# Attention stage of a hybrid encoder block: output-projection weights asked for two jobs ahead, residual rows one per unit, the first position table in its own pool

## The chip, the cores and the metric

The kernel runs on one core of one Trainium2 chip. The metric is the device time of one execution in microseconds (us), the median of three runs. Engines are named as in the profile: PE (TensorE matmul), DVE (VectorE), ACT (ScalarE), POOL (GpSimd) and SP (SyncE, which here only issues DMAs). Line numbers (L1020) are those of the kernel before.

## The reference, cut to what matters

One encoder layer over 1024 tokens of width 1024. One input projection feeds two groups of heads. The mLSTM group (4 heads of 128) gives `y_a`, the neighbourhood attention (8 heads of 64 on a grid of 16 rows by 64 columns, window 8 by 16) gives `y_b`; then come the output projection with the residual, an MLP and a gated embedding.

```python
s = jnp.einsum('bhcd,bhrcwd->bhcrw', q_row, k_win).astype(jnp.float32)
s = s + bias.transpose(0, 2, 1, 3)[None]          # rpb: learned position bias
prob = jax.nn.softmax(...)                        # over the 8 x 16 window
y_b = jnp.einsum('bhcrw,bhrcwd->bhcd', prob, v_win)
...
h = h + jnp.einsum('bse,ed->bsd', jnp.concatenate([y_a, y_b], axis=-1), w_out[i])
z = jnp.einsum('bsd,df->bsf', rms_norm(h, norm2_g[i]), w_ff1[i])
```

All products are made from fp32 values split into a high and a low part, with three matmuls for each product (`passes`).

## The kernel before, in words

The stages follow one another: input projections, mLSTM (pool `m1`), attention (pool `m2`), MLP, gate. The change lies in the attention stage, and in two lines at the end of the mLSTM stage.

The attention is cut into 32 units: `n = 8 pr + 4 rb + cb`, with four pairs of heads (`pr`), two row blocks and four column blocks. The order of the stage is written out by hand (`tc.manual_schedule()`, from L1102) and is pipelined by one unit. Unit n of the loop issues, in this order: `scores(n+1)` (six matmuls, L936), `values(n-1)` (twelve matmuls, L986), `prep_tiles(n)` (loads of the next pair's raw k and q rows, L836, and of its value tile `vw`, L894), `exps(n+1)` (DVE adds the position table to the scores and takes the extreme, L944; ACT the exponential, L945), `tab_load(n+5)` (the table five units ahead), `prep(n)` (in units 3, 4, 5, 9, 11 and so on: the next pair's k and q rows are normed on DVE, L817, with a small product `nb` on PE), a first portion of fill matmuls, `transposes(n)` (L966), the copies of the transposed probabilities (L973, L975) and the normalisation of unit n+1 (L950, L955, L957), and a second portion of fill matmuls.

A position table is a tile of 12 x 2 x 32 floats on 128 partitions. It comes in two DMAs (L923): half of the partitions from `tabI`, issued on SP, the other half from `tabU`, issued on POOL, and a memset on POOL (L924). In DRAM both are read as 4 x 16 pieces. Five tables are held (`TABS`), so table n+5 waits until `exps(n)` has read its buffer. The first table is loaded when the pool `m2` opens, in memory that the mLSTM stage has just left.

The fill matmuls are the output projection of the features that are ready (`out_part`, L1014), taken one at a time from the generator `fill_jobs`. There are six jobs: jobs 0 to 2 multiply the four mLSTM features (48 matmuls each), jobs 3 to 5 the first three attention features (36 each, possible from unit 24 on). FILLA and FILLB say how many are taken per portion, by pair of heads; the fill starts in unit 4. A job's weights `wo_...` are loaded by `w_raw` (L1020, on SP, three buffers) when the job before it starts, and split into high and low part by `w_split` (ACT L137, DVE L140) after that job's twelfth matmul. Both engines work in order, so a split that waits for its load holds up all that is behind it.

Beside that the first units hold: the last five row blocks of a v projection (`run(nv1, ...)`, 24 matmuls each, L309, and a store L342), the high/low split of the four mLSTM features (`y_split`, L1039 and L1040, units 2 and 3), and the loads of the residual rows (`out_res`, L1029, two at a time in units 2, 3 and 9).

SP issues its DMAs in program order, and each waits until the DMA issued eight before it on SP has landed (the eight completion counters go round), besides waiting for the buffer that it writes.

Of the kernel before, what the change touches and what calls it, by code (L numbers as in the profile page):

```python
# [18 lines left out]
P = 128  # L19
# [15 lines left out]
NV1 = 3  # L35
TABS = 5
PCS = 5
FILLA = (4, 4, 3, 7)
FILLB = (4, 4, 3, 7)
PREP0 = (0, 1, 2)  # L40
TBC = (1, 2, 3, 4)
ORD = ('n0', 'm1', 'n1', 'm2', 'n2', 'm3', 'n3', 'm0')
# [16 lines left out]
def tile_block(ctx, tc, xT, pT, w_in, w_out, w_ff1, w_ff2, w_gate, w_up, vecs, gate_b, rpbp, con,  # L59
# [391 lines left out]
    def run(it, n=None):  # L451
        for i, _ in enumerate(it):
            if n is not None and i == n - 1:
                return
# [222 lines left out]

    y_m = []
    aa, MP, wpv, wj, enm = (gk[n] for n in ("aa", "MP", "wpv", "wj", "enm"))
    m1p_ctx = tc.tile_pool(name="m1p", bufs=1, space=PSUM)  # L680
    m1p = m1p_ctx.__enter__()
    with tc.tile_pool(name="m1", bufs=2) as m1:

        heads = {}
# [183 lines left out]
        for h in range(4):  # L868
            mlstm_sweeps(h)
            if h == 0:  # L870
                na_ssq(7)
            if h < 3:
                mlstm_front2(h + 1)
                run(o0) if h == 0 else run(o1, 5) if h == 1 else run(o1)
            if h < 2:
                mlstm_front(h + 2)
            if h == 2:
                nv1 = proj_nv(1)
        run(nv1, NV1)
        with after("tk"):  # L880
            mlstm_finish(3)
# [7 lines left out]
    with tc.tile_pool(name="m2", bufs=2) as m2, tc.tile_pool(name="m2p", bufs=2, space=PSUM) as m2p:  # L889
# [7 lines left out]
        hres = {}  # L897


        NU = 32  # L900
        g3 = lambda t_: t_.rearrange("p (r c) -> p r c", c=64)
        heads2 = (slice(0, 64), slice(64, 128))
        tabs, scs, sms, pts, pvs, vws, ys = {}, {}, {}, {}, {}, {}, {}

        def geom(n):
            pr, u = divmod(n, 8)
            rb, cb = divmod(u, 4)
            return pr, rb, cb, KW[cb], 12 * KW[cb]

        def tab_load(n):  # L910
            if n >= NU:
                return
            pr, rb, cb, kw, w_ = geom(n)
            tab = m2.tile([P, 12, 2, 32], F32, tag="tab", name=f"tab{n}", bufs=TABS)
            tab = tab.rearrange("p a s b -> p (a s b)")[:, : 2 * w_]
            io, bo = (0, 64) if rb == 0 else (64, 0)
            r_0, a0, dead = (4, 0, 8) if rb == 0 else (0, 4, 0)
            k0 = (64 if cb > 1 else 0) + 16 * pr
            for q_, tb, p0, r0, c0, nr in ((nc.sync, tabI, io, 0, 0, 12), (nc.gpsimd, tabU, bo, r_0, a0, 8)):
                tb = tb[min(cb, 3 - cb)]  # L920
                src = bass.AP(tb.tensor, tb.offset + k0 * 30 * kw + r0 * 2 * kw,
                              [[2 * kw, 4], [30 * kw, 16], [1, nr * 2 * kw]])
                q_.dma_start(tab[p0 : p0 + 64, c0 * 2 * kw : (c0 + nr) * 2 * kw], src)  # L923
            G.memset(tab[bo : bo + 64, dead * 2 * kw : (dead + 4) * 2 * kw], NEG)  # L924
            tabs[n] = tab.rearrange("p (a s b) -> p s a b", s=2, b=kw)

        def scores(n):

# [94 lines left out]
        def w_split(raw, es, ks):  # L1023
            h_, l_ = split(wp, raw, raw.shape[1], "w", f"wo{ks[0]}_{es[0]}")
            return [t_.rearrange("p (k n) -> p k n", k=len(ks)) for t_ in (h_, l_)]
# [16 lines left out]
            ylo.append(b)  # L1042

        JOBS = [((e, e + 1), ks) for ks in (range(0, 4), range(4, 7)) for e in (0, 2, 4)]
        raws, ws_ = {}, {}

        def fill_jobs():
            for i, (es, ks) in enumerate(JOBS):
                if i + 1 < len(JOBS):
                    raws[i + 1] = w_raw(*JOBS[i + 1])  # L1050
                n = 0
                while len(yhi) <= ks[-1]:
                    yield
                for _ in out_proj(es, ks, mmps, ws_.pop(i)):
                    n += 1
                    if n == 12 and i + 1 < len(JOBS):
                        ws_[i + 1] = w_split(raws.pop(i + 1), *JOBS[i + 1])
                    yield

        fills = fill_jobs()  # L1060

# [38 lines left out]
                nat[pr + 1][2] = m2q(pr + 1, 0)  # L1100

        with tc.manual_schedule():  # L1102
            for n in range(TABS):
                tab_load(n)
                if n == 1:
                    vws[0] = load_vw(0)
            raws[0] = w_raw(*JOBS[0])
            scores(0)
            exps(0)
            for s in range(2):  # L1110
                recip(0, s)
                norm(0, s)
            for n in range(NU):
                if n + 1 < NU:
                    scores(n + 1)
                if n:
                    values(n - 1)
                prep_tiles(n)
                if n + 1 < NU:
                    exps(n + 1)  # L1120
                tab_load(n + TABS)
                begun = late[:]
                late.clear()
                for it in begun:
                    next(it, None)
                prep(n)
                for it in late:
                    next(it)
                if n:
                    values_out(n - 1, False)  # L1130
                if n < 4:
                    run(nv1, 1 if n < 2 else None)
                    if n > 1:
                        y_split(2 * n - 4)
                else:
                    fill(FILLA[n // 8])
                transposes(n)
                pt_copy(n, 1)
                if n + 1 < NU:
                    recip(n + 1, 0)  # L1140
                    norm(n + 1, 0)
                pt_copy(n, 0)
                if n + 1 < NU:
                    recip(n + 1, 1)
                    norm(n + 1, 1)
                if n:
                    values_out(n - 1, True)
                if n < 4:
                    run(nv1, 1) if n < 2 else None
                    if n > 1:  # L1150
                        y_split(2 * n - 3)
                    if n == 2:
                        ws_[0] = w_split(raws.pop(0), *JOBS[0])
                else:
                    fill(FILLB[n // 8])
                if n in (2, 3, 9):
                    e0 = {2: 0, 3: 2, 9: 4}[n]
                    out_res(e0)
                    out_res(e0 + 1)
            values(NU - 1)  # L1160
            values_out(NU - 1, False)
            values_out(NU - 1, True)
            run(fills)
    pj_ctx.__exit__(None, None, None)


# [497 lines left out]
```

## Time and profile before

| | us |
|---|---|
| median of 3 runs | 1435.9 (1429.86 to 1440.37) |
| the profiled execution | 1438.19 |
| its span, first to last instruction | 1436.4 |
| PE busy in the span | 1315.8 (92%) |
| attention stage, first scores to the start of unit 24 | 425.85 to 585.25 |

Times in the trace are us from the span's start. A "unit start" is the first `sc` matmul on L936 that the unit issues: unit 0 at 432.37 (its scores are those of unit 1), unit 7 at 494.53, unit 24 at 585.25. [...]

### The profile page before, as it was taken

Reading aid. Unit: us, or ns where it says so; the run is one execution under the profiler, and the core shown is the slowest. Engines: PE = TensorE matmul, PEld = TensorE weight load, DVE = VectorE, ACT = ScalarE, POOL = GpSimd, SP = SyncE. Lnnn points to the kernel's source line nnn. Section 1 sums busy time; section 2 is a strip of 40 time slices with the busy share of each in tenths; the row PEclk is TensorE's granted clock in tenths of the full one; section 3 lists DMA queues with packets and bytes.
Section 4 is the critical chain, followed back from the end, with each engine's and each line's share of the span. In section 5 each row is a group of like instructions: output and inputs, shape, how many; then the busy total and the mean of one; then the engine's idle time right before and its main releaser. Section 6 shows DMA issues by size and latency. Waiting matters only on the chain.

```text
span 1436.4 us, 19458 instructions
## 1 busy us (share of the span) xinstructions
PE 1315.8 (92%) x7055; PEld 1096.4 (76%) x7055; DVE 974.9 (68%) x1491; ACT 615.3 (43%) x1019; POOL 607.9 (42%) x481
## 2 busy tenths in 40 slices
PE   7999999999988669996999999999998899996887
PEld 6988777899877547774778888887886678885765
DVE  4487786665663436679756666666559987677788
ACT  7353443455554435545432333334333335445432
POOL 2215675553431213217266656653214640056654
PEclk9999999999998879998999999999999999998998
DMA  8543333565225544311244555446966754530152
GB/s 280 194 147 94 106 116 106 173 213 159 96 79 153 146 123 112 111 45 44 69 139 145 161 162 161 153 147 219 325 195 219 222 176 134 173 90 29 59 174 89
DMA packets 155344, 206.06 MB, mean 143 GB/s; under 512 B 20848, under 2 KB 104880, under 8 KB 155248
## 3 DMA queue, kind: packets, MB, share of 16 engines
q1 hardware_dynamic: 142480, 182.10, 40.4%
q10 hardware_dynamic: 7200, 13.11, 2.7%
q0 software_dynamic: 5568, 9.61, 2.3%
q8 instruction: 55, 0.90, 0.3%
q14 instruction: 41, 0.34, 0.1%
HBM read 151.60 MB, written 53.17 MB: 143 GB/s over the span
## 4 chain that ended last, share of the span: by engine, by line
PE 53%; DVE 11%; DMA 7%; issue 5%; POOL 4%; ACT 2%; SPq 0%; DVEq 0%; POOLq 0%; ACTq 0%
PE f_P L1364 14%; PE p_s_t L255 9%; PE p L255 5%; PE op L1014 4%; PE p_s L255 3%; PE p_t L255 3%; PE o0p L309 2%; PE pv L986 2%; PE o1p L309 1%; DMA wo_4r<-w_out 1%; PE pt L966 1%; PE num L754 1%; PE g_s L1489 1%; DMA tab<-tabI 1%; PE sc L936 1%
## 5 line engine op out<-in xcount | busy, mean ns | idle before, releaser
L1253 DVE TENSOR_TENSOR zl<-zr,zh 128x1024 fp32r<-128x1024 f32 x56 | 84.7, 1519 | 6.2 <-ACT zh L1252 6.2
L255 PE MATMUL p<-b,w_ah 128*128 128x512 f32 x256 | 80.4, 396 | 3.5 <-DVE b L192 3.5
L955 POOL TENSOR_SCALAR pc<-pc,st 128x288 f32<-128x288 f32 (+1 forms) x32 | 17.4, 542 | 150.6 <-DVE st L950 91.7
L1234 POOL TENSOR_TENSOR w2re<-sk,w2re 128x512 f32<-128x512 f32 x16 | 27.0, 1687 | 100.2 <-issue 69.1
L259 DVE TENSOR_TENSOR z<-z,p_s_t 128x512 f32<-128x512 f32 x64 | 42.5, 685 | 32.4 <-PE p_s_t L255 31.1
L1252 ACT ACTIVATE zh<-zr 128x1024 fp32r<-128x1024 f32 x56 | 58.2, 1047 | 11.7 <-DMA zr<-zd 10.8
L255 PEld LDWEIGHTS p<-b,w_ah 128*128 128x128 f32 x256 | 49.0, 192 | 14.1 <-DVE b L192 3.9
L1364 PE MATMUL f_P<-zl,w2h 128*128 128x512 f32 x128 | 51.8, 405 | 8.4 <-DVE zl L1253 8.4
L255 PE MATMUL p<-b,w_al 128*128 128x512 f32 x128 | 50.9, 399 | 7.6 <-DVE w_al L140 7.6
L986 PE MATMUL pv<-pT,vw 128*64 128x128 f32 (+1 forms) x384 | 30.1, 295 | 29.1 <-DVE pT L975 29.1
L945 ACT ACTIVATE pc<-pc,st 128x288 f32<-128x288 f32 (+1 forms) x64 | 36.3, 569 | 46.9 <-DVE st L944 46.9
L944 DVE CUSTOM_DVE_ANT_1 pc<-sc,tab 128x288 f32<-128x288 f32 (+1 forms) x64 | 29.9, 504 | 38.8 <-POOL pc L955 14.8
L1387 POOL TENSOR_TENSOR h<-h,evP 128x512 f32<-128x512 f32 x8 | 14.3, 1822 | 98.4 <-ACT evP L1378 98.4
L1277 POOL TENSOR_TENSOR tz<-z,z 128x512 f32<-128x512 f32 x16 | 20.7, 1296 | 82.4 <-ACT z L1266 82.4
L758 POOL TENSOR_SCALAR wv<-vh,wj 128x129 f32<-128x129 f32 x56 | 30.5, 549 | 56.1 <-PE num L759 50.8
L1364 PE MATMUL f_P<-zh,w2h 128*128 128x512 f32 x128 | 50.5, 394 | 1.1 <-ACT zh L1252 1.1
L1364 PE MATMUL f_P<-zh,w2l 128*128 128x512 f32 x128 | 50.4, 394 | 0.0
L1265 DVE SCALAR_TENSOR_TENSOR z<-z,Rb 128x1024 f32<-128x1024 f32 x32 | 49.3, 1547 | 0.9 <-ACT Rb L179 0.9
L986 PEld LDWEIGHTS pv<-pT,vw 128*64 128x64 f32 (+1 forms) x384 | 21.8, 144 | 36.6 <-DVE pT L975 30.6
L137 ACT ACTIVATE w_bh<-w_0r 128x1024 fp32r<-128x1024 f32 x16 | 17.0, 1062 | 74.4 <-POOL w_0r L233 54.7
L137 ACT ACTIVATE w_ah<-w_0r 128x1024 fp32r<-128x1024 f32 x16 | 17.0, 1062 | 68.4 <-PE p_t L255 68.4
L255 PE MATMUL p_s_t<-bt,w_bh 128*128 128x512 f32 x128 | 41.9, 410 | 3.4 <-ACT w_bh L137 3.4
(874 smaller groups left out, 4787.0 us busy)
## 6 DMA issues: line engine op xcount, KB each, us to landing
zr<-zd SPq DMA_DIRECT2D x56, 512.0 KB
zd<-z ACTq DMA_DIRECT2D x48, 256.0 KB
w2r<-w_ff SPq DMA_DIRECT2D x48, 256.0 KB
w_0r<-w_ff SPq DMA_DIRECT2D x16, 512.0 KB
w_1r<-w_ff SPq DMA_DIRECT2D x16, 512.0 KB
zd<-tz SPq DMA_DIRECT2D x32, 256.0 KB
zd<-z SPq DMA_DIRECT2D x32, 256.0 KB
w2re<-w_ff SPq DMA_DIRECT2D x16, 512.0 KB
```

Of the source, the lines that this page charges most:

```text
L137: mark["hi"] = S.activation(hi, raw, AF.Copy).ins
L255: TE.matmul(ps, x_, y_, start=j == 0 and i == 0, stop=j == 3 and i == 2)
L259: mark["add"] = V.tensor_tensor(o, a, b, op=ALU.add).ins
L309: mm = TE.matmul(ps[:, :256], a, b, start=k == 0 and i == 0, stop=k == KT - 1 and i == 2)
L758: G.tensor_scalar(wv, vh[:, c, 0:129], wj[:, col], 1.0, op0=ALU.mult, op1=ALU.mult)
L945: S.activation(pb, pb, AF.Exp, scale=-1.0, bias=st[:, 0:1], accum_out=st[:, 1:2])
L986: TE.matmul(pv[e0 : e0 + 64, cb], vws[pr][: 4 * kw, cb, rb + j, e0 : e0 + 64], pT[s][: 4 * kw, j], start=j == 0, stop=j == 2)
L1014: TE.matmul(ps, a, b, start=n == 0 and i == 0, stop=n == len(ks) - 1 and i == 2)
L1252: S.activation(hi, raw, AF.Copy)
L1253: dv.append(V.tensor_tensor(lo, raw, hi.bitcast(F32), op=ALU.subtract).ins)
L1265: V.scalar_tensor_tensor(z_, z_, 0.0, Rb, op0=ALU.max, op1=ALU.mult)
L1364: pe_last = TE.matmul(ps[n, e], a, b, start=st and k == 0, stop=sp and k == 2)
```

## The change

Job weights are loaded two jobs ahead: job 0's in unit 1, job 1's in unit 4, job 2's in unit 6, and each later one when the weights of the job two before it are split. A new function `job_weights`, called once per unit after the fill, makes the split when the running job has given at least twelve matmuls. The fill starts in unit 7 (NJ) with ten matmuls per unit, then ten in units 8 to 15, eight in units 16 to 23. The v projection's last five blocks are spread over units 0 to 3 (two, one, one, one), the four feature splits over units 3 to 6, and the residual rows are loaded one at a time in units 4, 5, 6, 7, 9 and 10. The first table has a pool of its own, opened before the mLSTM stage, and is loaded there; tables 5, 10, 15 ... use the same buffer, the others the remaining four. The `tabU` half of every table is issued on SP instead of POOL.

```diff
-FILLA = (4, 4, 3, 7)
-FILLB = (4, 4, 3, 7)
+FILLA = (5, 5, 4, 7)
+FILLB = (5, 5, 4, 7)
+NJ = 7
...
+    tb0_ctx = tc.tile_pool(name="tb0", bufs=1)
...
     def tab_load(n):
-            tab = m2.tile([P, 12, 2, 32], F32, tag="tab", name=f"tab{n}", bufs=TABS)
+        pool, tag, bufs = tabp[0] if n % TABS else (tb0, "tab0", 1)
+        tab = pool.tile([P, 12, 2, 32], F32, tag=tag, name=f"tab{n}", bufs=bufs)
...
-            for q_, tb, p0, r0, c0, nr in ((nc.sync, tabI, io, 0, 0, 12), (nc.gpsimd, tabU, bo, r_0, a0, 8)):
+        for q_, tb_, p0, r0, c0, nr in ((nc.sync, tabI, io, 0, 0, 12), (nc.sync, tabU, bo, r_0, a0, 8)):
...
             if h == 2:
                 nv1 = proj_nv(1)
+                tab_load(0)
...
         def fill_jobs():
             for i, (es, ks) in enumerate(JOBS):
-                if i + 1 < len(JOBS):
-                    raws[i + 1] = w_raw(*JOBS[i + 1])
-                n = 0
                 while len(yhi) <= ks[-1]:
                     yield
+                done[0] = 0
                 for _ in out_proj(es, ks, mmps, ws_.pop(i)):
-                    n += 1
-                    if n == 12 and i + 1 < len(JOBS):
-                        ws_[i + 1] = w_split(raws.pop(i + 1), *JOBS[i + 1])
+                    done[0] += 1
                     yield
+                cur[0] += 1
+
+        def job_weights():
+
+            i = cur[0] + 1
+            if done[0] >= 12 and i in raws and i not in ws_:
+                ws_[i] = w_split(raws.pop(i), *JOBS[i])
+                if i + 2 < len(JOBS):
+                    raws[i + 2] = w_raw(*JOBS[i + 2])
...
-            for n in range(TABS):
+            for n in range(1, TABS):
+                if n == 2:
+                    vws[0] = load_vw(0)
                 tab_load(n)
-                if n == 1:
-                    vws[0] = load_vw(0)
-            raws[0] = w_raw(*JOBS[0])
...
                 if n < 4:
-                    run(nv1, 1 if n < 2 else None)
-                    if n > 1:
-                        y_split(2 * n - 4)
-                else:
+                    run(nv1, 1 if n < 3 else None)
+                if n >= NJ:
                     fill(FILLA[n // 8])
...
-                if n < 4:
-                    run(nv1, 1) if n < 2 else None
-                    if n > 1:
-                        y_split(2 * n - 3)
-                    if n == 2:
-                        ws_[0] = w_split(raws.pop(0), *JOBS[0])
-                else:
+                if n < 1:
+                    run(nv1, 1)
+                if n >= NJ:
                     fill(FILLB[n // 8])
-                if n in (2, 3, 9):
-                    e0 = {2: 0, 3: 2, 9: 4}[n]
-                    out_res(e0)
-                    out_res(e0 + 1)
+                if 3 <= n < 7:
+                    y_split(n - 3)
+                if n == 6:
+                    ws_[0] = w_split(raws.pop(0), *JOBS[0])
+                job_weights()
+                if n in (1, 4, 6):
+                    j = {1: 0, 4: 1, 6: 2}[n]
+                    raws[j] = w_raw(*JOBS[j])
+                if n in (4, 5, 6, 7, 9, 10):
+                    out_res({4: 0, 5: 1, 6: 2, 7: 3, 9: 4, 10: 5}[n])
```

SP's queue before, from the second pair of residual rows on (`tab_4804` is table 9, `wo_2r` the weights of job 1, `h` residual rows, `nvd` the last v store):

```order
L342 DMA nvd<-nv1t_4680 128x2x128
L1029 DMA h_4711<-xT 128x1024
L1029 DMA h_4713<-xT 128x1024
L923 DMA tab_4739<-tabI_111 64x1x576
L1029 DMA h_4778<-xT 128x1024
L1029 DMA h_4780<-xT 128x1024
L923 DMA tab_4804<-tabI_112 64x1x768
L1020 DMA wo_2r<-w_out 128x4x256
L923 DMA tab_4876<-tabI_112 64x1x768
```

The same place of SP's queue in the changed kernel (`tab_4783` is table 9):

```order
L343 DMA nvd<-nv1t_4738 128x2x128
L708 DMA tab_4783<-tabI_112 64x1x768
L708 DMA tab_4783<-tabU_114 64x1x512
L1029 DMA wo_2r<-w_out 128x4x256
L1038 DMA h_4825<-xT 128x1024
L708 DMA tab_4852<-tabI_112 64x1x768
L708 DMA tab_4852<-tabU_114 64x1x512
L1038 DMA h_4888<-xT 128x1024
L708 DMA tab_4912<-tabI_111 64x1x576
L708 DMA tab_4912<-tabU_113 64x1x384
```

The load of job 1's weights still stands right behind table 9. The four residual loads that stood ahead of it now stand behind it, and every table has a second DMA on this queue.

ACT before, unit 5 (`pc_0_4868` holds the scores of unit 6, `pT_1_4908` the transposed probabilities of unit 5):

```order
L945 ACTIVATE pc_0_4868,st_0_4869<-pc_0_4868,st_0_4869 128x384
L945 ACTIVATE pc_1_4872,st_1_4873<-pc_1_4872,st_1_4873 128x384
L830 ACTIVATE qh_0_4866<-nr_4641 128x512
L137 ACTIVATE wo_2h<-wo_2r 128x1024
L973 ACTIVATE pT_1_4908<-pt_1_4904 128x384
L957 ACTIVATE pc_0_4868<-pc_0_4868,st_0_4869 128x384
```

ACT in the changed kernel, unit 8 (`pc_0_5014` holds the scores of unit 9):

```order
L954 ACTIVATE pc_0_5014,st_0_5015<-pc_0_5014,st_0_5015 128x384
L954 ACTIVATE pc_1_5018,st_1_5019<-pc_1_5018,st_1_5019 128x384
L1007 ACTIVATE yh_4799<-pv_1_4835 128x4x8x16
L982 ACTIVATE pT_1_5042<-pt_1_5038 96x384
L966 ACTIVATE pc_0_5014<-pc_0_5014,st_0_5015 128x384
L138 ACTIVATE wo_2h<-wo_2r 128x1024
```

The split of job 1's weights moved from the middle of unit 5 to the end of unit 8, behind the copies and the normalisation of its unit.

## Rows read from the trace of the kernel before

**Rows 1.** Chain that ended last, 395 to 540: start us, us, what.

```profile
425.64 5.79 DMA tab<-tabU
...
444.05 10.68 DMA nvd<-nv1t
...
460.95 14.51 DMA tab<-tabI
...
475.47 11.23 DMA wo_2r<-w_out
...
511.30 16.80 DMA wo_4r<-w_out
```

**Rows 2.** Waits, 414 to 540: who waited for whom, total us, times, longest.

```profile
ACT wo_4h L137 <- DMA wo_4r<-w_out: 12.2, 1, 12.2
...
ACT wo_2h L137 <- DMA wo_2r<-w_out: 9.1, 1, 9.1
```

**Rows 3.** PE's timeline: start us, us, engine, line, operation [idle before <- releaser].

```profile
432.37 1.06 PE L936 MATMUL sc<-kh,q 64*128 64x384 f32 x2 [5.86 <-DVE st L944]
...
489.62 1.55 PE L986 MATMUL pv<-pT,vw 128*64 128x128 f32 x12 [10.11 <-DVE pT L975]
...
494.53 0.40 PE L936 MATMUL sc<-kh,qh 64*128 64x288 f32 x2
...
498.65 0.45 PE L936 MATMUL sc<-kh,qh 64*128 64x384 f32 x2
...
531.01 1.55 PE L986 MATMUL pv<-pT,vw 96*64 96x128 f32 x12 [13.09 <-DVE pT L975]
...
581.61 0.40 PE L936 MATMUL sc<-kh,qh 64*128 64x288 f32 x2
...
585.25 0.45 PE L936 MATMUL sc<-kh,qh 64*128 64x384 f32 x2
```

**Rows 4.** Windows of 3 us: PE, PEld, DVE, ACT, POOL busy (x), PEclk, DMA share, GB/s.

```profile
429.00:432.00 3.00, 0.00 (x0) 0.00 (x0) 0.15 (x1) 0.00 (x0) 1.01 (x3) 0.50 0.78 185
432.00:435.00 3.00, 2.63 (x10) 2.11 (x11) 1.69 (x9) 1.65 (x6) 1.13 (x3) 0.50 0.28 84
480.00:483.00 3.00, 0.00 (x0) 0.00 (x0) 0.00 (x0) 0.00 (x0) 0.00 (x0) 0.91 0.26 94
483.00:486.00 3.00, 0.00 (x0) 0.00 (x0) 0.00 (x0) 0.00 (x0) 0.00 (x0) 0.50 0.27 89
507.00:510.00 3.00, 3.00 (x27) 2.12 (x26) 1.69 (x7) 1.69 (x5) 1.47 (x3) 1.00 0.96 243
519.00:522.00 3.00, 0.00 (x0) 0.00 (x0) 0.00 (x0) 0.00 (x0) 0.00 (x0) 0.66 0.26 101
540.00:543.00 3.00, 3.00 (x27) 2.50 (x24) 2.80 (x8) 2.17 (x7) 0.00 (x0) 1.00 0.27 66
```

**Rows 5.** DMA issues, 380 to 660: what, queue, count, KB each, median us to landing (POOL's).

```profile
tab<-tabI SPq DMA_DIRECT2D x16, 192.0 KB
tab<-tabI SPq DMA_DIRECT2D x16, 144.0 KB
tab<-tabU POOLq DMA_DIRECT2D x16, 128.0 KB, 6.5
vw<-nvd SPq DMA_DIRECT2D x8, 256.0 KB
tab<-tabU POOLq DMA_DIRECT2D x16, 96.0 KB, 5.7
vw<-nvd SPq DMA_DIRECT2D x8, 192.0 KB
```

**Rows 6.** SP's queue, 404 to 540: start us, us, line, what, count.

```profile
500.29 2.43 SPq L894 DMA_DIRECT2D vw<-nvd  x4
```

**Rows 7.** DVE's timeline, first reduction of scores in units 1 and 23, as rows 3.

```profile
447.49 0.56 DVE L944 CUSTOM_DVE_ANT_1 pc<-sc,tab 128x384 f32<-128x384 f32 x1 [7.59 <-PE pt L966]
...
582.40 0.46 DVE L944 CUSTOM_DVE_ANT_1 pc<-sc,tab 128x288 f32<-128x288 f32 x1 [0.99 <-POOL pc L955]
```

More of the change, by code (lines that the diff above doesn't have):

```diff
@@ L679, in tile_block, with geom, tab_load @@
     aa, MP, wpv, wj, enm = (gk[n] for n in ("aa", "MP", "wpv", "wj", "enm"))
+    tb0_ctx = tc.tile_pool(name="tb0", bufs=1)
+    tb0 = tb0_ctx.__enter__()
     m1p_ctx = tc.tile_pool(name="m1p", bufs=1, space=PSUM)
     m1p = m1p_ctx.__enter__()
+    NU = 32
+    tabs, tabp = {}, []
+    def geom(n):
+        pr, u = divmod(n, 8)
+        rb, cb = divmod(u, 4)
+        return pr, rb, cb, KW[cb], 12 * KW[cb]
+    def tab_load(n):
+        if n >= NU:
+            return
+        pr, rb, cb, kw, w_ = geom(n)
+        pool, tag, bufs = tabp[0] if n % TABS else (tb0, "tab0", 1)
+        tab = pool.tile([P, 12, 2, 32], F32, tag=tag, name=f"tab{n}", bufs=bufs)
+        tab = tab.rearrange("p a s b -> p (a s b)")[:, : 2 * w_]
+        io, bo = (0, 64) if rb == 0 else (64, 0)
+        r_0, a0, dead = (4, 0, 8) if rb == 0 else (0, 4, 0)
+        k0 = (64 if cb > 1 else 0) + 16 * pr
+        for q_, tb_, p0, r0, c0, nr in ((nc.sync, tabI, io, 0, 0, 12), (nc.sync, tabU, bo, r_0, a0, 8)):
+            tb_ = tb_[min(cb, 3 - cb)]
+            src = bass.AP(tb_.tensor, tb_.offset + k0 * 30 * kw + r0 * 2 * kw,
+                          [[2 * kw, 4], [30 * kw, 16], [1, nr * 2 * kw]])
+            q_.dma_start(tab[p0 : p0 + 64, c0 * 2 * kw : (c0 + nr) * 2 * kw], src)
+        G.memset(tab[bo : bo + 64, dead * 2 * kw : (dead + 4) * 2 * kw], NEG)
+        tabs[n] = tab.rearrange("p (a s b) -> p s a b", s=2, b=kw)
     with tc.tile_pool(name="m1", bufs=2) as m1:
@@ L897, in tile_block @@
         hres = {}
-        NU = 32
         g3 = lambda t_: t_.rearrange("p (r c) -> p r c", c=64)
         heads2 = (slice(0, 64), slice(64, 128))
[L903 to L913, printed above, removed]
-            tab = m2.tile([P, 12, 2, 32], F32, tag="tab", name=f"tab{n}", bufs=TABS)
[L915 to L918, printed above, removed]
-            for q_, tb, p0, r0, c0, nr in ((nc.sync, tabI, io, 0, 0, 12), (nc.gpsimd, tabU, bo, r_0, a0, 8)):
[L920 to L925, printed above, removed]
+        tabp.append((m2, "tab", TABS - 1))
+        scs, sms, pts, pvs, vws, ys = {}, {}, {}, {}, {}, {}
         def scores(n):
@@ L1044, in tile_block @@
         JOBS = [((e, e + 1), ks) for ks in (range(0, 4), range(4, 7)) for e in (0, 2, 4)]
-        raws, ws_ = {}, {}
+        raws, ws_, done, cur = {}, {}, [0], [0]
         def fill_jobs():
             for i, (es, ks) in enumerate(JOBS):
-                if i + 1 < len(JOBS):
-                    raws[i + 1] = w_raw(*JOBS[i + 1])
-                n = 0
                 while len(yhi) <= ks[-1]:
                     yield
+                done[0] = 0
                 for _ in out_proj(es, ks, mmps, ws_.pop(i)):
-                    n += 1
-                    if n == 12 and i + 1 < len(JOBS):
-                        ws_[i + 1] = w_split(raws.pop(i + 1), *JOBS[i + 1])
+                    done[0] += 1
                     yield
+                cur[0] += 1
[5 more added lines that the diff above has]
+                    raws[i + 2] = w_raw(*JOBS[i + 2])
         fills = fill_jobs()
@@ L1162, in tile_block @@
             values_out(NU - 1, True)
-            run(fills)
+            for _ in fills:
+                job_weights()
+    tb0_ctx.__exit__(None, None, None)
     pj_ctx.__exit__(None, None, None)
```

## The prediction, made before the run

> **What bounds the stage now.** I read the chain of waits first. In the attention stage it is not made of PE work alone: five DMA pieces stand in it [rows 1]. The list of waits names the two that the change speaks of, ACT's splits of the weights `wo_2` and `wo_4`, 9.1 and 12.2 us [rows 2]. PE's timeline gives what they cost there: 10.11 and 13.09 us of idle PE, and 5.86 us more in front of unit 0, where DVE waits for the first table (its POOL half landed 5.79 us after its issue) [rows 1, 3]. Between the stalls PE sets the pace: unit 7 takes 4.12 us with eight fill matmuls, unit 23 3.64 us with six, so a fill costs 0.24 us; units 7 to 23 took 4.57 us each in the mean, the second stall left out [rows 3].
>
> Then I asked why those loads take 11.23 and 16.80 us to land [rows 1], and read the windows. While PE stood idle for `wo_2`, the DMA engines were busy at a share of 0.26 and 0.27 and moved 94 and 89 GB/s; for `wo_4` it was 0.26 and 101 GB/s. With residual rows and weights in flight the share was 0.96 at 243 GB/s [rows 4]. A share that stays near 0.25 is four of the 16 engines at work. With only tables asked for on SP (540 to 543) it is 0.27 as well [rows 4]. So the tables and, by the same share in 432 to 435, the value tiles run on four engines, and the weights' last pieces wait there behind them. While the POOL halves of the first five tables landed (429 to 432) the share was 0.78 [rows 4]: those were spread wider.
>
> I take from this a sum for the four engines. What runs on them alone moves at 96 GB/s (the windows at 94, 89 and 101). A DMA of 512 KB over all 16 engines costs them between 1.33 us (a quarter of its bytes at 96) and 2.9 us. The upper end is from `wo_4`: from the issue of the value tile at 500.29 [rows 6] to 528.10 are 27.8 us; less 1.7 us of start and end, 12.8 us for 1232 KB of tile and tables, and 1.8 us for POOL's table halves, 11.5 us are left for four such DMAs. I take 2.0, near the 2.1 us that 512 KB take at the 243 GB/s of the busy window.
>
> The sum tried on the kernel before: up to `wo_2` the queue holds tables 0 to 9 (1680 KB of `tabI`), two value tiles (each 2 x 192 and 2 x 256 KB [rows 5], 1792 KB together) and 9.5 DMAs' worth of 512 KB: 427 + 3472/96 + 19 + 1 = 483.2, where 427 is the first data, 1.4 us after the first table issue, and 1 us is the completion. It landed at 486.70. The 3.5 us missing are the ten POOL halves, which use these engines too.
>
> **The change part by part.**
>
> *Weights and splits.* The two waits of rows 2 go if the loads land before their new place. The load of `wo_2` keeps its place in the queue (behind table 9), but is needed at the end of unit 8. By the sum it lands at 427 + (2560 + 1792)/96 + 5.25 x 2.0 + 1 = 483.8 (tables 1 to 9, two value tiles). Unit 5 goes on at 472.5 (below), and three and a half units at 4.57 us later unit 8 ends at about 488. `wo_4` lands at 427 + (3120 + 1792)/96 + 8.25 x 2.0 + 1 = 495.7 and is needed at the end of unit 12, four units later, about 507. So these waits cost nothing more: at most 23.2 us are free.
>
> *Fill moved.* 24 fill matmuls leave units 4 to 6 and come back in units 7 to 22: 5.8 us of PE that move. Without them units 3 to 6 are paced by DVE and by loads. The feature splits (1.2 us of DVE each) are spread over them, no work is added.
>
> *The first table early.* It is loaded in the mLSTM stage, beside PE work; I cost it at nothing there. Bounds: nothing, and 2.5 us if a load of that stage waits behind its 240 KB. Unit 0 then starts near 427.5 instead of 432.37. What is late next is table 2: in the kernel before DVE takes up the scores of unit 2 at 447.49, 4 us after PE has made them. The row puts that to PE, but no work of that unit needs the transposes; table 2 is what is left. Changed, it lands at 427 + 1536/96 + 1 = 444. So of the 4.9 us won in unit 0, 3.5 are still there in unit 1.
>
> *The second half of the tables on SP.* This is the part that speaks against the change. It takes 32 issues off POOL, which is not on the path, and puts 96 or 128 KB per table [rows 5] on the queue whose four engines are the slow ones. The trace has no `tabU` on SP; the nearest row is `tabI`, read in the same 4 x 16 pieces. At `tabI`'s rate a table costs 2.5 or 3.3 us of the four engines instead of 1.5 or 2.0 and POOL's 0.35. If SP spread it like POOL does, it would cost 1.9 or 2.4. I take the first, since it is the same shape on the same queue.
>
> [...]
>
> *SP as a queue.* Each SP DMA waits for the one eight before. With 32 more this means about 11 us from issue to landing at the rate above; tables are issued five units (over 20 us) ahead, so it holds nothing back as long as the four engines keep up.
>
> *The sum.* Needed until unit 23 can reduce its scores is table 24. In the queue up to it: tables 1 to 24, 12 x 320 + 12 x 240 = 6720 KB; four value tiles, 3584 KB; and 9472 KB over all engines (six loads of k and q rows, six of residual rows, three weights of 512 KB, three of 384, five stores of 128), 18.5 x 512 KB. 10304/96 = 107.3 and 18.5 x 2.0 = 37.0: it lands at 427 + 107.3 + 37.0 + 1 = 572.3. Two reductions follow and unit 24 starts at 573.6, against 585.25 [rows 3]; in the kernel before DVE began these reductions at 582.40 [rows 7]. On the way the waits fall after each value tile: q rows in unit 5 at 472.5, in unit 13 at 525.7, in unit 21 at 565.8. From 525.7 PE alone, ten units at 4.57 us, would reach unit 24 at 571.4: both paces end together. From unit 24 on both kernels do the same, at 14 fills per unit, paced by PE.
>
> So 11.7 us are won: 1438.2 - 11.7 = 1426.5 for an execution like the profiled one, which lies 2.3 us above the median; against the median 1435.9 - 11.7 = 1424.
>
> **The rivals.**
>
> *The queue does not pace the stage.* If SP spreads the second halves, or the four engines are faster than the windows say, nothing takes the place of the three waits: 5.86 + 10.11 + 13.09 = 29 us less, 1407. For it: after unit 13 the kernel before shows no long wait for a DMA. Against it: 0.26 at 94 and 89 GB/s with all compute engines idle, so the queue alone was late there.
>
> *The queue becomes the bound and is slower than summed.* With both halves on one queue the four engines have work from 427 to 572 without a gap. If they run at the 84 GB/s of 432 to 435 [rows 4], and a DMA over all engines costs them 2.9 us, the sum grows by 122.7 - 107.3 + 18.5 x 0.9 = 32 us, and the time is 1456: the wait has moved from the weights to the tables and the k and q rows. It turns slower than before where the 144.3 us of service grow by more than 11.7, that is by 8%. For it: `wo_4`'s 2.9 us, and that busy engines are slow (243/16 = 15 GB/s each, against 24 when four work). Against it: the engines also lose POOL's packets, and the check on `wo_2` came out within 3.5 us.
>
> *The waits on weights stay in part*, because `wo_2` lands after unit 8: its margin is only 4 us. This is within the forecast, since tables 9 and 10 are as late then.
>
> **How the numbers follow.** The forecast has 0.58, the first rival 0.27, the slower one 0.15. The forecast's own range: at 1.33 us per DMA the sum is 12 us shorter, but PE's pace holds the gain at some 23 us (1413); at 2.9 us it is 17 us longer (1441). The range reaches from 1404, a little past the first rival, to 1441; the end of the slower rival is left out. A measurement of this kernel tells about 1% from no change, that is 14.4 us. Faster by more has the first rival nearly whole and some 0.2 of the forecast where the four engines do better than 2.0: 0.46. Slower by more is the far third of the slower rival: 0.06. Within 1%: 0.48.
>
> **What would show it.** Right: no ACT wait of several us for `wo_2` or `wo_4`, no 5.86 us ahead of unit 0; long DMA pieces in the chain that end in tables or k and q rows, in units 1, 5, 13 and 21; a DMA share seldom under 0.25 between 427 and 570; unit 24 near 574. The first rival shows as units 7 to 22 at PE's pace throughout, and unit 24 before 560. The slower one shows as DVE waiting for a table in nearly every unit. I would be wrong in the mechanism if unit 1 took up its scores before 440, or if two halves of a table on SP showed a share of 0.5.

## Result: 1421.9 us, 14 us less, and the profile after

| | before | after |
|---|---|---|
| median of 5 runs, us | 1435.9 (1429.9 to 1440.4) | 1421.9 (1420.7 to 1424.5) |
| the profiled execution, its span | 1438.2, 1436.4 | 1421.5, 1419.7 |
| PE busy between 427 and 570 | 108.5 | 126.5 |
| scores of unit 24, of unit 31 after the first scores | 155.8, 192.1 | 143.6, 179.9 |

The ratio is 0.9906, 95% interval 0.9878 to 0.9935, which is 9 to 18 us less; forecast were 1424 and 11.7 us. Since the stage starts at different times in different executions (last section), I count inside it from the middle pass of the first scores (`sc<-kl`, 426.08 before, 425.98 after) and call this stage time. "Scores of unit n" is the stage time of the same pass in unit n. At the scores of unit 31 the changed kernel is 12.3 us ahead (192.13 - 179.87). The two spans differ by 16.7; the other 4.3 us come after these scores, in code that the change hardly touches, and are of the size by which executions differ there (last section).

The chain of the changed kernel, 395 to 600 us (start, us, what), which answers to [rows 1]:

```profile
430.04 13.53 DMA tab<-tabU
...
458.99 12.32 DMA nr<-qnd
...
509.71 13.98 DMA nr<-qnd
...
550.10 12.59 DMA tab<-tabU
```

The weights are gone from the chain. In their place stand two tables and two loads of q rows (`nr`), all four asked for on SP behind a value tile: a late transfer again, but another one. The list of waits (414 to 540, total us, times, longest) has no wait for a weight's load any more [rows 2]; what comes first among the DMAs is

```profile
DVE pc L953 <- DMA tab<-tabU: 18.0, 4, 10.0
...
POOL pc L964 <- DMA nr<-qnd: 7.1, 1, 7.1
...
DVE nr L847 <- DMA nr<-qnd: 5.4, 3, 3.7
```

PE's timeline, with the idle time before a row in brackets, answers to [rows 3]:

```profile
425.98 0.29 PE L945 MATMUL sc<-kl,q 64*128 64x288 f32 x2
...
427.06 0.82 PE L945 MATMUL sc<-kh,q 64*128 64x384 f32 x2 [0.66 <-DVE st L953]
...
444.35 1.08 PE L945 MATMUL sc<-kh,q 64*128 64x288 f32 x2 [2.79 <-DVE st L953]
...
521.94 0.88 PE L945 MATMUL sc<-kh,qh 64*128 64x288 f32 x2 [3.11 <-DVE st L953]
...
525.71 1.55 PE L995 MATMUL pv<-pT,vw 128*64 128x128 f32 x12 [2.63 <-DVE pT L984]
...
572.09 0.82 PE L945 MATMUL sc<-kh,qh 64*128 64x384 f32 x2 [0.45 <-DVE st L953]
```

The 5.86 us ahead of unit 0 are 0.66, the 10.11 and 13.09 are gone; instead 2.79 stand at the start of unit 2, 3.11 and 2.63 in unit 14, and unit 24 starts at 572.09 (585.25 before; 573.6 forecast). DVE's timeline says for what PE waited there (the reductions of the scores of units 2 and 14, the first with the wait of [rows 7], and the q rows of units 5 and 13):

```profile
443.73 0.56 DVE L953 CUSTOM_DVE_ANT_1 pc<-sc,tab 128x384 f32<-128x384 f32 x1 [9.96 <-DMA tab<-tabU]
...
471.41 0.75 DVE L847 SCALAR_TENSOR_TENSOR nr<-nr,qgs,nb 128x512 f32<-128x512 f32 x1 [0.89 <-DMA nr<-qnd]
...
521.31 0.56 DVE L953 CUSTOM_DVE_ANT_1 pc<-sc,tab 128x384 f32<-128x384 f32 x1 [5.98 <-DMA tab<-tabU]
...
523.78 0.75 DVE L847 SCALAR_TENSOR_TENSOR nr<-nr,qgs,nb 128x512 f32<-128x512 f32 x1 [0.82 <-DMA nr<-qnd]
```

Windows of 3 us, columns as in [rows 4] (the last three are PEclk, PE's granted clock as a share of full speed, the mean busy share of the 16 DMA engines, and GB/s):

```profile
435.00:438.00 3.00, 3.00 (x31) 2.44 (x31) 0.00 (x0) 0.47 (x1) 0.00 (x0) 1.00 0.26 102
...
501.00:504.00 3.00, 3.00 (x38) 2.42 (x37) 0.87 (x5) 1.17 (x5) 0.34 (x2) 1.00 0.27 100
504.00:507.00 3.00, 3.00 (x19) 2.31 (x19) 0.51 (x1) 0.00 (x0) 0.00 (x0) 1.00 0.26 98
...
519.00:522.00 3.00, 0.06 (x1) 0.07 (x1) 0.69 (x3) 0.09 (x1) 0.00 (x0) 1.00 0.26 104
...
525.00:528.00 3.00, 2.29 (x14) 1.87 (x15) 2.08 (x9) 1.93 (x6) 0.84 (x2) 0.50 0.55 182
```

In the first of these windows nothing but tables and a value tile is in flight, in the next three also the last pieces of wide loads (k, q or residual rows). The share is 0.26 or 0.27 in these four, though both halves of the tables are now on SP: the halves joined the same quarter of the engines. In the windows of 3 us from 429 to 573 the share is never under 0.25, so the queue has no gap. The last row shows the aftermath of a wait: PE has work again, at a granted clock of 0.50. In the kernel before it was the same behind the wait for `wo_4`:

```profile
531.00:534.00 3.00, 2.99 (x28) 2.85 (x28) 2.17 (x7) 1.44 (x5) 1.42 (x3) 0.50 0.15 15
```

So a wait costs somewhat more than its idle time: twelve value matmuls take 1.55 us behind the waits ([rows 3], and 525.71 above), and 0.88 in the changed kernel at 497.19, in a window (495 to 498) at 1.00.

### The profile page after: what moved, and what is told of

The parts are those of the page before. It is cut to its first block, busy times and chain, and to the rows that moved or that the text cites. A ratio compares the mean times of both kernels' runs of the same rounds, so it can differ in the third digit from the quotient of the medians.

```text
span 1419.7 us, 19412 instructions
## 1 busy us (share of the span) xinstructions
PE 1315.6 (93%) x7055; PEld 1095.2 (77%) x7055; DVE 976.4 (69%) x1491; ACT 613.9 (43%) x1019; POOL 586.3 (41%) x449
## 4 chain that ended last, share of the span: by engine, by line
PE 52%; DVE 13%; DMA 6%; issue 5%; POOL 3%; ACT 2%; SPq 0%; DVEq 0%; POOLq 0%; ACTq 0%
PE f_P L1379 14%; PE p_s_t L256 9%; PE p L256 6%; PE op L1023 4%; PE p_s L256 3%; PE p_t L256 3%; DMA nr<-qnd 2%; DMA tab<-tabU 2%; PE o0p L310 2%; PE pv L995 1%; PE o1p L310 1%; DVE h L1402 1%; PE g_s L1504 1%; PE num L784 1%; DVE zl L1268 1%
## 5 line engine op out<-in xcount | busy, mean ns | idle before, releaser
L954 ACT ACTIVATE pc<-pc,st 128x288 f32<-128x288 f32 (+1 forms) x64 | 36.3, 569 | 57.9 <-DVE st L953 57.9
L1281 ACT ACTIVATE z<-z 128x1024 f32<-128x1024 f32 x32 | 33.9, 1060 | 22.0 <-DVE z L1280 21.8
L141 DVE TENSOR_TENSOR w_cl<-w_1r,w_ch 128x1024 fp32r<-128x1024 f32 x16 | 23.1, 1444 | 29.2 <-ACT w_ch L138 29.0
```

The source lines that it names most:

```text
L954: S.activation(pb, pb, AF.Exp, scale=-1.0, bias=st[:, 0:1], accum_out=st[:, 1:2])
L1281: S.activation(z_, z_, AF.Square)
```

## The experiments

My theory: tables and value tiles on SP share four DMA engines, and this queue sets the end of the stretch from the stage's start to unit 13. Rivals: the queue lands just in time and compute engines set the pace; SP as an issuing queue is what is slow; each wait costs on its own. In the table, "scores 14" and "scores 31" are the scores of these units, and "q rows" is the stage time at which DVE takes the q rows of unit 13. The ratios are to the kernel before as it was timed beside each kernel (medians 1434.8 to 1438.0), so they are not quotients of the medians shown.

| kernel | scores 14 | q rows | scores 31 | median us | ratio to before, 95% |
|---|---|---|---|---|---|
| before | 112.4 | | 192.1 | 1435.9 | |
| the change | 87.5 | 97.8 | 179.9 | 1421.9 | 0.9906 (0.9878 to 0.9935) |
| u_pool | 87.2 | 91.3 | 170.6 | 1413.5 | 0.9844 (0.9813 to 0.9874) |
| t0_late | 87.8 | 98.2 | 180.3 | 1423.2 | 0.9904 (0.9878 to 0.9930) |
| vw_rows | 87.4 | 93.6 | 174.6 | 1418.0 | 0.9868 (0.9843 to 0.9893) |
| b_u_sp | 117.0 | | 199.0 | 1442.5 | 1.0033 (1.0010 to 1.0056) |
| t0_m2 | 89.9 | 100.2 | 181.4 | 1423.7 | 0.9905 (0.9876 to 0.9935) |
| w_only | 88.0 | 96.0 | 176.8 | 1418.2 | 0.9862 (0.9837 to 0.9887) |
| u_rows | 83.9 | 90.6 | 171.5 | 1415.9 | 0.9846 (0.9819 to 0.9872) |
| u_pool_vw_rows | 84.0 | 87.4 | 167.3 | 1407.4 | 0.9787 (0.9761 to 0.9814) |
| h_late | 87.5 | 93.5 | 180.2 | 1423.0 | 0.9904 (0.9873 to 0.9936) |
| y_late | 89.6 | 97.3 | 179.0 | 1422.3 | 0.9896 (0.9862 to 0.9929) |
| best | 80.4 | 84.4 | 163.6 | 1406.9 | 0.9785 (0.9753 to 0.9816) |
| vw_after_q | 90.3 | 93.6 | 178.0 | 1419.1 | 0.9886 (0.9859 to 0.9913) |

**The halves back on POOL (u_pool).**

```diff
-(nc.sync, tabU, bo, r_0, a0, 8)
+(nc.gpsimd, tabU, bo, r_0, a0, 8)
```

> The changed kernel, but the second half of every table is asked for on POOL's queue again. Four-engine theory (tables and value tiles on SP share four DMA engines, and those set the pace): a table costs these engines 1.17 us less for its half and 0.35 us more for POOL's packets, 0.82 us less; after six tables the q rows that unit 5 needs land near 466 instead of 471.3, after 14 those of unit 13 near 512 instead of 523.7, and from there PE's pace (4.57 us per unit) leads to unit 24 near 563 instead of 572.2: 1412 us, range 1408 to 1416, clearly faster than the changed kernel's 1422. Rival 1 (the queue only lands in time, PE and DVE set the pace): 1422, within 3 us. Rival 2 (the half on SP is itself a gain, because POOL's issues stand ahead of the scaling of the probabilities and the NEG fills that others wait for): 1424 to 1430, and waits of DVE and PE for POOL grow.

1413.5 us, the q rows of unit 13 6.5 us earlier, the scores of unit 31 9.2 us earlier. So the halves on SP cost the change about 8 to 9 us. The time came as expected, but not at the place I named first: the q rows of unit 5 were taken at 470.6, where 466 was expected, those of unit 13 at 516.2 instead of 512, and up to the scores of unit 14 both kernels run alike (87.5 and 87.2). From there to unit 25 u_pool takes 50.0 us for eleven units (87.2 to 137.3), 4.55 each, PE's pace. What DVE waits for the q rows of unit 13 is under a microsecond:

```profile
516.20 0.75 DVE L847 SCALAR_TENSOR_TENSOR nr<-nr,qgs,nb 128x512 f32<-128x512 f32 x1 [0.66 <-DMA nr<-qnd]
```

**One part of the change on the kernel before (b_u_sp):** the second halves on SP, in L923's loop, nothing else.

```diff
-(nc.gpsimd, tabU, bo, r_0, a0, 8)
+(nc.sync, tabU, bo, r_0, a0, 8)
```

> The kernel before with one part of the change alone: the second half of every table on SP. Four-engine theory: ten tables ahead of the weight load that unit 7 waits for, 0.5 to 0.8 us each: it lands 5 to 8 us later than 486.7, and the one of unit 13 7 to 11 us later than 528.1; after that PE sets the pace: 1443 to 1447 us, 1445 the middle. Rival 1 (the half spreads on SP as on POOL, or the queue does not pace): 1436, within 3 us. Rival 2 (POOL relieved is a gain): 1432 or less.

1442.5, just under the expected range, slower by 0.33% (interval 0.10 to 0.56). ACT's timeline:

```profile
486.34 1.06 ACT L137 ACTIVATE wo_2h<-wo_2r 128x1024 fp32r<-128x1024 f32 x1 [10.36 <-DMA wo_2r<-w_out]
...
528.61 1.06 ACT L137 ACTIVATE wo_4h<-wo_4r 128x1024 fp32r<-128x1024 f32 x1 [12.15 <-DMA wo_4r<-w_out]
```

This execution's stage begins at 420.88, so the weights come at stage times 65.5 and 107.7; in the kernel before (426.08; 486.73 and 528.12) at 60.7 and 102.0. They are 4.8 and 5.7 us later, where I expected 5 to 8 and 7 to 11.

**Table 0 late (t0_late, then t0_m2).** The first edit only moved the call:

```diff
-                tab_load(0)
-            for n in range(1, TABS):
+            for n in range(TABS):
```

> The changed kernel, but table 0 is asked for at the start of the attention stage, ahead of table 1. Four-engine theory: 240 KB more go through the four engines in the stage, 2.5 us at 96 GB/s, and every later landing moves by that: table 2 near 446, the q rows of unit 5 near 474, of unit 13 near 526, unit 24 near 575: 1424.5 us, range 1423 to 1427; the wait in front of unit 0 returns (some 4 us) but most of it is swallowed in front of table 2. Rival (each wait costs on its own): the whole wait of 5.4 us (the start of unit 0, 432.6 against 427.2) returns, unit 24 near 577.5, 1427.5 us.

Nothing moved (1423.2), and SP's timeline shows why: the load is still issued in the mLSTM stage.

```profile
305.35 0.68 SPq L708 DMA_DIRECT2D tab<-tabI  x1
```

What lets it go early is not the line that asks for it but the pool of its own. So the run answered nothing about the wait, and the second edit took the pool away and gave its buffer to the pool of the other tables:

```diff
-        pool, tag, bufs = tabp[0] if n % TABS else (tb0, "tab0", 1)
+        pool, tag, bufs = tabp[0]
```

> The changed kernel, but table 0 has its place in the pool of the other tables, which is laid over memory of the mLSTM stage, so its load can't start before that stage has let go; all five tables rotate in that pool. All times from the first scores of the stage. Theory A (from unit 12 on the four-engine queue sets the pace, so a wait at the start is partly swallowed): the scores of the second unit start 6 us after the first instead of 1.5 (as in the kernel before), those of the 15th at 91 to 93 instead of 87.5, but the q rows of unit 13 come only 2.5 us (240 KB at 96 GB/s) later: unit 24 and the end 2.5 us later, 1424.5 us, range 1423 to 1426. Rival (each wait costs on its own): the whole 5 us stay to the end, 1427 us.

The wait is back (the scores of unit 1 at 5.7 instead of 1.5), at unit 14 2.4 us of it are left (89.9, where 91 to 93 were expected), the q rows come 2.4 us later, and at the end 1.5 us remain; 1423.7. In the changed kernel the early table is worth 4.2 us where it acts and 1.5 us at the end, since the queue swallows the rest.

**The weights alone (w_only):** u_pool's and t0_m2's edits together.

> Of the change only the weights, residual rows, splits and fills are left: table 0 in the pool of the others as in the run before this one, and the second halves of the tables on POOL's queue as in the kernel before. Theory A (the weight waits are what the change takes away, the first table gives a few us more, the halves on SP take 8 back): no ACT wait for a weight, the wait ahead of the second unit's scores is back, unit 13 waits for its q rows by less than 2 us: 1417 us, range 1415 to 1420, about 4 us above the run with only the halves back on POOL (1413.5), still under the changed kernel. Rival (the weight waits go only because the halves on SP or the early table change what the queue holds): a wait of ACT for a weight of 3 us or more is back, 1424 or more.

No wait for a weight in the list, 1418.2, as theory A said, though unit 13 waits longer than the 2 us I allowed (DVE 3.64 for a table and 0.84 for the q rows, which come at 96.0 against 91.3 in u_pool). With the other runs this takes the change apart, in stage time at unit 31: weights, residual rows, splits and fills, which moved together and which no run parts, 192.1 to 176.8, 15.3 us less; the second halves on SP cost 4.5 (176.8 to 181.4); the early table gives 1.5 (181.4 to 179.9). In the other order the table gives 6.2 (176.8 to 170.6) and the halves cost 9.2 (170.6 to 179.9): the parts don't add up independently, since both act on one queue. The first table's wait itself is not the same either: with the halves on POOL the scores of unit 1 come at 8.5 (w_only), with the halves on SP at 5.7 (t0_m2).

**Which property of SP is it? (vw_rows, u_rows)** Smaller pieces of the same bytes on the same queue: value tiles in 16 DMAs instead of four, or the second half of each table as four DMAs of 16 rows.

```diff
-                nc.sync.dma_start(vw[0 : 4 * KW[cb], cb], nvd[:, KC0[cb] : KC0[cb] + KW[cb], pr])
+                for r in range(4):
+                    nc.sync.dma_start(vw[r * KW[cb] : (r + 1) * KW[cb], cb], nvd[r, KC0[cb] : KC0[cb] + KW[cb], pr])
```

> The changed kernel, but each value tile is loaded by 16 DMAs of 24 or 32 rows each instead of four of 96 or 128 rows whose slowest DRAM dimension is 4. Four-engine theory: a tile then spreads over 12 or 16 engines and costs the four engines some 3.5 us (896 KB at 2.0 us per 512 KB) instead of 9.3, 5.8 us less per tile; with two tiles ahead the q rows of unit 5 land near 460, the wait in unit 13 goes, PE's pace leads to unit 24 near 558 to 562: 1410 us, range 1406 to 1414, and windows with a tile show a share well over 0.26. Rival 1 (the pieces stay on the four engines): same landings, 1422, share 0.26 while a tile loads. Rival 2 (twelve more issues per tile hold up SP, where each DMA waits for the one eight before): tables behind a tile are asked for some 5 us later, 1424 to 1428.

```diff
+                for i in range(4):
+                    si = bass.AP(tb_.tensor, tb_.offset + k0 * 30 * kw + r0 * 2 * kw + i * 2 * kw,
+                                 [[30 * kw, 16], [1, nr * 2 * kw]])
+                    q_.dma_start(tab[p0 + 16 * i : p0 + 16 * i + 16, c0 * 2 * kw : (c0 + nr) * 2 * kw], si)
```

> The changed kernel, the second half of every table still on SP, but asked for as four DMAs of 16 rows each, whose slowest dimension is 16 instead of 4. Four-engine theory: these halves spread over 16 engines and cost the four slow ones some 0.45 us instead of 1.17; the q rows of unit 13 land 6 to 10 us earlier after the first unit's scores than in the changed kernel and the time comes near that of the run with the halves on POOL: 1415 us, range 1412 to 1418. Rival (SP's queue itself is what is slow: its issues and its rule that each DMA waits for the one eight before): 96 more issues make every load later, 1428 us or more, with waits for tables in many units.

u_rows: 1415.9 and the q rows 7.2 us earlier, with 96 more issues on SP. So not the issuing queue but the few engines were slow. A window in which tables and the first value tile alone are in flight, in u_rows and then in the changed kernel, shows the wider spread:

```profile
432.00:435.00 3.00, 3.00 (x28) 3.00 (x26) 0.73 (x3) 1.75 (x5) 0.83 (x2) 1.00 0.50 128
```

```profile
432.00:435.00 3.00, 3.00 (x28) 3.00 (x27) 1.27 (x6) 2.55 (x7) 0.83 (x2) 1.00 0.26 101
```

The second half of a table is the same bytes in both. With it in pieces of 16 rows the window has a share of 0.50 at 128 GB/s, with it in one DMA read as 4 x 16 pieces 0.26 at 101. How many engines a single DMA takes no run shows, so neither the 16 of this expectation nor the 12 or 16 of the one before, on which its 3.5 us per tile rest; what vw_rows showed in their place stands below.

vw_rows won less than expected, 1418.0 instead of 1410: three tiles should have cost 17 us less by unit 13, and the q rows came 4.2 us earlier. Some of the 17 us could not show there: the scores of unit 14 come at 87.4, hardly earlier than in the changed kernel, and where DVE waits little for these rows (u_pool) it takes them 4.1 us behind those scores. For the rest SP's queue gives a reason; the third value tile of the changed kernel and of vw_rows:

```profile
496.21 8.25 SPq L925 DMA_DIRECT2D vw<-nvd  x4
```

```profile
493.65 15.32 SPq L926 DMA_DIRECT2D vw<-nvd  x16
...
510.79 0.37 SPq L866 DMA_DIRECT2D nr<-qnd  x1
```

Sixteen small loads took 15.3 us to ask for, and the q rows stand behind them. The first tile, in 426 to 436, took 9.85 us, no less than its 896 KB cost four engines at 96 GB/s (9.3); the share was 0.46 and 0.51 in the windows from 426 to 432, but at only 109 and 125 GB/s. Here the rival that I had priced as a loss did act. How much of the gain it took back is not separated: in u_pool_vw_rows the third tile takes as long (15.29), and the q rows come at 87.4 all the same.

**Both relieved (u_pool_vw_rows),** the edits of u_pool and vw_rows together.

> The changed kernel with the second halves of the tables on POOL's queue and the value tiles in 16 DMAs of 24 or 32 rows. Theory A (with the halves on POOL the queue no longer sets the pace after unit 13: 4.55 us per unit there, which is PE's own): nothing is left to win there, only the first three units can gain by the faster tile, 0 to 3 us: 1412 us, range 1410 to 1414. Rival (the four engines still hold something back in most units): another 5 us or more less, 1408 or under.

1407.4, the time of the rival; but the stage moved as theory A said: from unit 14 to 31 it takes 83.3 us, u_pool 83.4, and the 3.3 us of gain lie ahead of unit 14. The rest of the 6.2 us between the two medians is not seen in the stage of the profiled executions.

**A bound that the queue hides (y_late).** In the changed kernel DVE waits four times, 6.0 us together, for ACT's half of a feature split, with the next reductions behind it. The edit moves DVE's half behind them (the new function `y_low` holds the removed line):

```diff
-            V.tensor_tensor(b, y_m[h], a.bitcast(F32), op=ALU.subtract)
...
+                if 4 <= n < 8:
+                    y_low(n - 4, low)
                 tab_load(n + TABS)
```

> The changed kernel, the DVE half of the four feature splits taken from the end of units 3 to 6 to behind the score reductions of the unit after, so that DVE no longer waits for ACT ahead of these reductions (6.0 us in four waits in the changed kernel). Two bounds stand against each other in units 3 to 13. If the four-engine queue sets the end of that stretch: units 4 to 9 are 3 to 6 us shorter, the q rows of unit 13 still land at 97 to 98 after the first scores, and the end of the stage stays, 1421 us, range 1419 to 1423. Rival (DVE and ACT set the stretch, and the queue only lands beside it): all of the 3 to 6 us stay to the end, 1416 to 1418 us.

The scores of unit 9 come at 57.9 instead of 60.6, 2.7 us earlier; those of unit 14 at 89.6 instead of 87.5; the q rows at 97.3 instead of 97.8; 1422.3. Most of what was won goes into longer waits for the k rows of unit 11 (6.04, 3.70 in the changed kernel) and the q rows of unit 13 (1.07, 0.82 there):

```profile
506.33 0.75 DVE L847 SCALAR_TENSOR_TENSOR nr<-nr,vec,nb 128x512 f32<-128x512 f32 x1 [6.04 <-DMA nr<-qnd]
...
523.43 0.75 DVE L847 SCALAR_TENSOR_TENSOR nr<-nr,qgs,nb 128x512 f32<-128x512 f32 x1 [1.07 <-DMA nr<-qnd]
```

Compute that ends earlier waits longer: in this stretch the queue sets the end.

**What a load over all engines costs (h_late).** Four loads of residual rows come later, by which three fewer stand ahead of those q rows.

```diff
-                if n in (4, 5, 6, 7, 9, 10):
-                    out_res({4: 0, 5: 1, 6: 2, 7: 3, 9: 4, 10: 5}[n])
+                if n in (4, 5, 10, 11, 14, 15):
+                    out_res({4: 0, 5: 1, 10: 2, 11: 3, 14: 4, 15: 5}[n])
```

> The changed kernel, three of the six loads of residual rows (512 KB each, over all 16 engines) asked for in units 11, 14 and 15 instead of 6, 7 and 9, so that they no longer stand ahead of the q rows of unit 13. It measures what one such load costs the four engines. All times from the first scores of the stage; in the changed kernel DVE takes these q rows at 97.8. Four-engine theory at my 2.0 us each: they land 6 us earlier, 91.8 (94 at the low bound of 1.33, 89 at the high one of 2.9; DVE can take them from about 91 on, when the unit is there); the end of the stage 4 to 6 us earlier, 1417 us, range 1415 to 1420. Rival (loads over 16 engines go beside the tables at next to no cost): landing at 97 to 98, 1422 us.

DVE takes the q rows at 93.5 without a wait, 4.3 us or more earlier: at least 1.4 us for each of the three loads, so not free; whether 2.0 is right this run can't say (the landings below can). The time did not fall (1423.0), a miss: I had moved the rows past the point where they are needed, and DVE waited for them one unit later.

```profile
524.56 0.69 DVE L1025 TENSOR_TENSOR h<-h,op 128x512 f32<-128x512 f32 x1 [3.43 <-DMA h<-xT]
```

**The order of the queue (vw_after_q),** the value tiles behind the q rows instead of ahead of them.

```diff
                 krs[pr + 1] = raw_load(2 * pr + 3, m2, "kr", 1)
-                vws[pr + 1] = load_vw(pr + 1)
...
                 qrs[pr + 1] = raw_load(2 * pr + 2, m2, "qr", 1)
+                vws[pr + 1] = load_vw(pr + 1)
```

> The changed kernel, the value tiles of the second to fourth pair asked for behind the q rows (units 2, 10, 18) instead of behind the k rows (units 1, 9, 17). The same DMAs on the same queue, in another order. Four-engine theory (the queue has no gap from the stage's start to unit 13, so its total counts and not the order): the q rows of unit 13 and table 14 land some 9 us earlier (a tile is 896 KB at 96 GB/s), but table 15, now behind the tile, lands where it did: DVE takes the scores of unit 15 100 to 101 us after the first scores, as now (100.7), after a wait of 5 us or more for a table; 1421 us, range 1419 to 1423. Rival (what is late is only these q rows and table 14, the rest has slack): the waits of units 12 and 13 go and nothing comes in their place, 8 us less, 1412 to 1415.

The q rows come 4.2 us earlier and without a wait, and table 15 is late in their stead:

```profile
521.61 0.46 DVE L953 CUSTOM_DVE_ANT_1 pc<-sc,tab 128x288 f32<-128x288 f32 x1 [4.65 <-DMA tab<-tabI]
```

With this stage's first scores at 421.39 that is 100.2, within the 100 to 101 expected, after a wait a little under the 5 us expected. At unit 31 1.9 us are won; 1419.1. What the queue holds in all decides, its order hardly.

**The version that beats both (best):** the edits of u_pool, vw_rows and y_late, and the first value tile behind table 2.

```diff
-                if n == 2:
+                if n == 3:
                     vws[0] = load_vw(0)
```

> The second halves of the tables on POOL's queue, value tiles in 16 DMAs, the feature splits as in the run before this one, and the first value tile asked for behind table 2 instead of ahead of it. With the queue relieved, what is left to win is in the first nine units, where DVE waits 8.6 us for table 2 (PE idle about 3) and four times for a feature split. Theory: both are PE time here, since nothing later absorbs it: 3 us by table 2 and 3 to 6 by the splits, against 1407.4: 1400 us, range 1397 to 1403. Rival (another wait of the queue takes their place, the value tile itself or the k rows): 1405 to 1409.

1406.9: the scores of unit 31 at 163.6, 3.7 us earlier than without the last two edits, where 6 to 9 were expected, and no more than half a microsecond by the medians. Against u_pool_vw_rows it is not shown faster; against the kernel before both are 2.1% less, and their intervals lie clear of the changed kernel's.

## Why the prediction was right, point by point

- *Weight waits.* Right: they are gone, and w_only gives the gain of the weights with the residual rows, splits and fills that moved along, 15.3 us at unit 31. The margins were larger than forecast: `wo_2` is split at 490.85, some 7 us after its landing (below).
- *First table.* Right: unit 0 waits 0.66 us, and table 2 is next: forecast to land at 444, taken at 443.73.
- *Halves on SP.* Right, and the largest cost in the change: the share stayed at 0.26, and undoing this part alone makes the kernel 8 us faster.
- *The sum of the queue.* Right within 2 us at each landing: q rows of unit 5 forecast 472.5, taken 471.4; of unit 13 525.7 and 523.8; unit 24 573.6 and 572.1. Two of its terms no row gives, the 1.4 us from the first issue to the first data and the 1 us of completion. In the trace of the kernel before the first table is issued at 425.13 and the first data moves at 426.55, 1.4 us later, so the sum's start of 427 is 0.4 late; the last data of `wo_2` moves just before 486.0 and it lands at 486.70, so the completion takes 0.7 to 0.8 us. The two weights show in SP's own waits (480 to 496):

```profile
SPq L866 <- DMA wo_4r<-w_out: 1.0, 1, 1.0
SPq L1038 <- DMA wo_2r<-w_out: 0.9, 1, 0.9
```

The DMA that is eight places behind `wo_2` is issued at 483.68 and the one behind `wo_4` at 494.65, each after a wait for that landing; forecast were 483.8 and 495.7. This lets me estimate both prices apart. Table 2 has no wide load ahead of it: 1536 KB by 443.6, which with the forecast's start and completion is 98 GB/s. At 96 GB/s `wo_2` then leaves 2.0 us for each of its 5.25 wide loads, and `wo_4` 1.9 for each of 8.25. The trial on the kernel before had 9.5 wide loads, where SP's queue holds 9.25 (eight of 512 KB and five stores of 128); half a microsecond more is then left to the POOL halves.
- *Where the waits fall.* Units 1 and 13 as forecast. In unit 5 the q rows did land last, but by under a microsecond: u_pool, with its queue relieved, is no faster up to unit 14, so something else needs as long there. For the feature splits y_late shows it, 2.7 us by unit 9; that the rest is the other work of PE, DVE and ACT in these units is not shown. The forecast's half sentence that units 3 to 6 are paced by DVE and by loads weighed too little there. In unit 21 DVE waits 2.87 us for a table, but PE only 0.64, and the q rows are taken at 564.41 without a wait (forecast 565.8): PE was already at its own pace, as the sum had it ("both paces end together").
- *The first rival,* 1407, needed a queue that doesn't pace the stage. It does; but relieved of it, in u_pool_vw_rows, the kernel takes 1407.4. In the stage that is 24.8 us of the rival's 29 (192.1 to 167.3), so the equal number is in part chance.
- *The size.* Forecast 11.7 us, measured 12.3 in the stage and 14.0 by the medians. The stage is what was summed; the further 1.7 us have no cause in the forecast and are within the spread between executions, so that they point the same way is luck.

## What to carry to other kernels

Where a load lands late, ask how many of the DMA engines it runs on: here a busy share that stayed near 0.25 with idle compute meant a narrow pattern, and moving more transfers onto the same queue cost 8 to 9 us. The full queue swallowed gains ahead of it (2.7 us became 0.5) and passed a removed wait on to its next customer, so sum its bytes up to each point of need, and reorder only after the sum is smaller. Splitting narrow transfers into wide ones won 6 us for the table halves (u_rows) and 4 for the value tiles (vw_rows), where asking for the pieces became the new queue.

## What was not expected of the hardware

Between profiled executions the stage began anywhere from 420.0 to 426.9 us and the program ran another 813.9 to 818.2 us after the scores of unit 31, with no edit in these parts to which that could be put. The changed kernel has the lowest of the latter times and the kernel before the highest. For the start it goes in part with the granted clock; the window 200 to 220, far ahead of any edit, in the changed kernel and in t0_late (PE busy first, PEclk third from the end):

```profile
200.00:220.00 20.00, 18.29 (x71) 14.50 (x72) 13.55 (x16) 5.13 (x6) 11.12 (x7) 0.83 0.66 203
```

```profile
200.00:220.00 20.00, 19.12 (x82) 15.06 (x83) 14.61 (x18) 6.20 (x7) 11.29 (x6) 1.00 0.54 170
```

One execution had a stretch at a lower clock there and the other not; their stages begin at 425.98 and 420.89. Of the fourteen executions the six at 0.83 in this window begin the stage at 424.8 to 426.9, the five at 1.00 at 420.0 to 425.2, so the clock there is not the whole of it. These differences are as large as several of the effects above, so parts of a few microseconds were read from stage times and not from spans. Why a drop comes in one execution and not in another stays open.
